# Far passes of a two-buffer sort in four instructions, one rotation less, other counts of zero matmuls

## The chip, the cores and the metric

The kernel runs on one core of a Trainium2 chip. The metric is the device time of one execution in microseconds (us). Before the change three runs took 396.53, 396.72 and 397.1 us; the median is 396.72.

## The reference

4096 nodes have 256 features each. Each of 262144 edges carries its source node's features, times a weight matrix, to its target node, where they are summed; each node's own features, times a second matrix, are added.

```python
self_out = nodes @ w_self
src_feat = nodes[edges_src]
msg = src_feat @ w_msg
agg = np.zeros((N, D), dtype=np.float32)
np.add.at(agg, edges_dst, msg)
return (self_out + agg).astype(np.float32)
```

## The kernel before

Nothing is gathered edge by edge. Each edge becomes one key, and the keys are sorted by a shell sort on the chip until each chunk of 128 edges touches one block of sources and a narrow window of targets. The main stage, from about 150 us on, makes one-hot matrices of the chunks on VectorE (DVE), multiplies them on TensorE (PE) into counts per block and window (`ring`), evicts these on ScalarE (ACT) and multiplies them with the projected nodes `Y` into `out_ps`. Two tables of 2048 numbers each, `WID` and `GAP`, give the columns that each chunk's window may take; they follow from the sort's amounts.

The sort holds 128 x 2048 keys in one of two buffers, `XA[0]` and `XA[1]`, and goes from one to the other. A pass with a distance m compares each key of every second block with the key m further on in the same partition: one DVE instruction writes the minima and one the maxima (`mm`, line 1156). Two passes of the same m, with parity 0 and 1, are a pair. Pairs of m over 96 (`FP`) are far passes, the others near passes. `SORT_A` (line 202) lists the passes, and between them rotations (`'q'`).

- Far passes: `far_gap` (line 1237) does a pair in seven DVE instructions and leaves untouched blocks where they are, in a buffer that it writes in part. ACT has no part in it. `far_pass` (line 1258) is not reached, since all far passes come in pairs.
- Near passes: `near` (line 1212) does all pairs between two rotations. It cuts the passes into waves, so that the first half of the array is ready for the next rotation while DVE still works on the second. It also calls `warm`.
- Rotations: `rotate` (line 1275) turns each half by 8 groups of matmuls with a shifted identity, in three PSUM tiles, each copied back by ACT. The next near passes start on the first half when it has been copied.
- `warm` (line 1162) puts groups of n zero matmuls (128 x 512) into PE's order ahead of the next rotation, each made to wait for the DVE instruction that lies a given span before the point at which the first half is ready. `WARM` (line 176) has for each rotation the spans and n.

The order of each engine is the order of the code (`manual_schedule`); waits are on semaphores that the framework derives from the data. Work that the sort doesn't need is put between its parts by a generator, `early` (line 487): 16 steps that transpose the nodes (four matmuls into `x_ps` and a cast to `XT`), then 32 projections into `Y` and 16 of the nodes' own rows (two matmuls into `y_ps` and a copy each). `FILLS` (line 178) says how many steps come ahead of the sort and behind each rotation. `x_ps` and `y_ps` share two PSUM buffers. After the sort come a transposition (`relayout`), a tail of 14 near passes on each half of the keys (one half at once, the other beside the main stage), and the main stage.

Of the kernel before, what the change touches and what calls it, by code (L numbers as in the profile page):

```python
# [11 lines left out]
P = 128  # L12
# [160 lines left out]
BEFORE, AFTER = 0, 2  # L173
FP = 96
BP = 128
WARM = [((6.0, 4.8, 3.6, 2.4, 1.2), 3)] + [((2.7, 1.4), 3)] * 8
TURNED = ((0, 4), (4, 2), (6, 2))
FILLS = (24, 10, 10, 10, 0, 5, 0, 0, 5)
LAG = (16, 84)
# [83 lines left out]
def kernel(  # L263
# [86 lines left out]
    j = 0  # L350
# [148 lines left out]
    for _ in range(FILLS[0]):  # L499
        next(fill)  # L500
# [902 lines left out]
```

## Time and profile before

| | |
|---|---|
| median of three runs | 396.72 us |
| profiled execution: time / span | 396.69 / 394.8 us |
| DVE busy | 356.4 us (90%) |
| PE busy | 321.8 us (82%) |
| ACT busy | 261.2 us (66%) |
| POOL busy | 77.9 us (20%) |
| mean granted PE clock | 0.985 |

Busy times are of the whole span; the stages differ. In the sort and its tail, to about 145 us, DVE is busy nearly all the time. In the main stage PE, DVE and ACT share the work, and PE has the most of it. The clock is that of PE, as a share of full speed.

### The profile page before, as it was taken

Reading aid. Unit: us, or ns where it says so; the run is one execution under the profiler, and the core shown is the slowest. Engines: PE = TensorE matmul, PEld = TensorE weight load, DVE = VectorE, ACT = ScalarE, POOL = GpSimd, SP = SyncE. Lnnn points to the kernel's source line nnn. Section 1 sums busy time; section 2 is a strip of 40 time slices with the busy share of each in tenths; the row PEclk is TensorE's granted clock in tenths of the full one; section 3 lists DMA queues with packets and bytes.
Section 4 is the critical chain, followed back from the end, with each engine's and each line's share of the span. In section 5 each row is a group of like instructions: output and inputs, shape, how many; then the busy total and the mean of one; then the engine's idle time right before and its main releaser. Section 6 shows DMA issues by size and latency. Waiting matters only on the chain.

```text
span 394.8 us, 11312 instructions
## 1 busy us (share of the span) xinstructions
PE 321.8 (82%) x4147; PEld 274.1 (69%) x4157; DVE 356.4 (90%) x616; ACT 261.2 (66%) x571; POOL 77.9 (20%) x1088
## 2 busy tenths in 40 slices
PE   0028688886967188998999899999999999999985
PEld 0016256664746054987898798989999989999974
DVE  5999999999999998899999999979999899999350
ACT  4418155533447105868897879999888888888862
POOL 5499950000000100000200202120212020211001
PEclk9999999999999779999999999999999999999999
DMA  8691000011032400000301202221121112121204
GB/s 302 155 185 28 3 2 0 5 49 55 1 107 69 146 0 2 2 2 2 42 2 16 28 2 30 56 38 21 17 29 18 25 17 30 15 28 18 28 2 71
DMA packets 17731, 16.26 MB, mean 41 GB/s; under 512 B 3334, under 2 KB 16647, under 8 KB 17674
## 3 DMA queue, kind: packets, MB, share of 16 engines
q0 software_dynamic: 8992, 6.29, 13.4%
q1 hardware_dynamic: 7962, 7.22, 5.3%
q10 hardware_dynamic: 720, 2.00, 1.4%
q8 instruction: 34, 0.56, 0.6%
q14 instruction: 23, 0.19, 0.2%
HBM read 8.93 MB, written 8.67 MB: 45 GB/s over the span
## 4 chain that ended last, share of the span: by engine, by line
DVE 45%; PE 45%; ACT 5%; issue 2%; DMA 1%; ACTq 0%; DVEq 0%
PE out_ps L890 21%; DVE XA L1158 20%; PE ring L795 17%; DVE oh L766 9%; DVE XR L1158 6%; DVE XS L1158 4%; DVE off L729 3%; PE tp_sw L1284 3%; PE warm L1178 3%; ACT XA L1288 2%; ACT atr L823 2%; DMA d<-in_edges_dst_dram 1%; PE out_ps L897 1%; DVE XA L392 1%; DVE XA L387 1%
## 5 line engine op out<-in xcount | busy, mean ns | idle before, releaser
L823 ACT CAST atr<-ring 128x468 bf16<-128x468 f32 (+15 forms) x352 | 170.2, 559 | 30.7 <-PE ring L795 30.2
L890 PE MATMUL out_ps<-Y,atr 128*128 128x256 bf16 x1024 | 149.9, 272 | 0.6 <-ACT o_sb L907 0.5
L766 DVE TENSOR_SCALAR oh<-off 128x2560 bf16<-128x2560 int16 (+8 forms) x209 | 132.9, 694 | 8.4 <-PE ring L795 6.2
L795 PE MATMUL ring<-oh 128*128 128x70 bf16 (+23 forms) x2048 | 112.4, 197 | 7.0 <-issue 4.5
L795 PEld LDWEIGHTS <-oh 128*128 128x128 bf16 x2048 | 104.5, 98 | 15.6 <-issue 8.3
L890 PEld LDWEIGHTS <-atr 128*128 128x128 bf16 x1024 | 97.1, 98 | 7.7 <-issue 0.2
L1158 DVE TENSOR_TENSOR XA<-XA 128x510 f32<-128x510 f32 (+32 forms) x154 | 89.4, 631 | 2.5 <-ACT XA L1288 0.5
L795 PE MATMUL ring<-zer 128*128 128x156 bf16 (+13 forms) x352 | 80.9, 231 | 1.1 <-ACT atr L823 0.9
L1048 POOL DMA_DIRECT2D out_dram<-o_sb x30 | 32.9, 1130 | 217.0 <-ACT atr L823 217.0
L1288 ACT COPY XA<-tp_sw 128x256 f32<-128x256 f32 (+1 forms) x48 | 19.8, 450 | 37.5 <-PE tp_sw L1284 37.2
L1284 PE MATMUL tp_sw<-XA,id 128*128 128x128 f32 x256 | 32.4, 278 | 6.8 <-DVE XA L1158 6.3
L729 DVE TENSOR_TENSOR off<-pair,rows 128x2560 int16<-128x2560 int16 (+5 forms) x28 | 37.6, 1344 | 0.3
L1284 PEld LDWEIGHTS tp_sw<-XA,id 128*128 128x128 f32 x256 | 30.0, 190 | 11.2 <-DVE XA L1158 9.0
L795 PEld LDWEIGHTS <-zer 128*128 128x128 bf16 x358 | 34.6, 97 | 2.7 <-ACT atr L823 1.4
L1178 PE MATMUL warm<-zw 128*128 128x512 bf16 x78 | 23.7, 412 | 15.3 <-DVE XS L1158 9.1
L443 POOL MEMSET prow<- 1x1 f32 x1024 | 33.9, 89 | 1.2 <-issue 1.2
L479 PE MATMUL x_ps<-id_bf,nodes_bf 128*128 128x128 bf16 x64 | 8.5, 303 | 28.7 <-DMA nodes_bf<-in_nodes_dram 27.5
L897 PE MATMUL out_ps<-Y,atr 128*82 128x256 bf16 (+9 forms) x115 | 31.3, 272 | 0.0
L754 ACT ACTIVATE oh<-off,onesc 128x640 bf16<-128x640 uint16 (+5 forms) x30 | 22.7, 760 | 8.6 <-DVE off L729 7.2
L479 PEld LDWEIGHTS <-nodes_bf 128*128 128x128 bf16 x64 | 6.6, 139 | 30.4 <-DMA nodes_bf<-in_nodes_dram 27.8
L1178 PEld LDWEIGHTS <-zw 128*128 128x128 bf16 x87 | 8.0, 101 | 27.6 <-DVE XS L1158 9.4
L451 PE MATMUL y_ps<-wcat,XT 128*128 128x256 bf16 x128 | 22.3, 286 | 5.6 <-ACT Y L455 2.2
(115 smaller groups left out, 231.4 us busy)
## 6 DMA issues: line engine op xcount, KB each, us to landing
out_dram<-o_sb POOLq DMA_DIRECT2D x30, 128.0 KB, 3.3
nodes_bf<-in_nodes_dram POOLq DMA_DIRECT2D x2, 1024.0 KB, 12.3
out_dram<-nodes_bf SPq DMA_DIRECT2D x4, 512.0 KB, 3.8
out_dram<-XA SPq DMA_DIRECT2D x4, 512.0 KB, 3.1
s<-in_edges_src_dram ACTq DMA_DIRECT2D x2, 512.0 KB
d<-in_edges_dst_dram SPq DMA_DIRECT2D x2, 512.0 KB, 5.4
s<-in_edges_src_dram ACTq DMA_DIRECT2D x1, 480.0 KB, 9.2
d<-in_edges_dst_dram SPq DMA_DIRECT2D x1, 480.0 KB, 9.4
```

Of the source, the lines that this page charges most:

```text
L443: nc.gpsimd.memset(words[:, z0:z1], float(packed[z0]))
L729: tt(out=v[:, 0:n // 2].rearrange("p g w (k i) -> p (g w) k i", i=2), in0=pair[:, g].rearrange("p g w i -> p (g w) i").unsqueeze(2).to_bro ...
L766: ins = tss(out=bass.AP(tensor=dst.tensor, offset=dst.offset, ap=[list(row), [2 * WE, n // 2], [2 * P, both], [1, 2 * NW]],), in_=v[:, 0:n ...
L795: mm = nc.tensor.matmul(out=ap, lhsT=lhsT, rhs=rhs, start=start, stop=True, skip_group_check=True,).ins
L823: ins = nc.scalar.copy(out=atr[:, i:i + k, 0:n], in_=_view3(ring[:, b:b + k * BW], BW)[:, :, 0:n]).ins
L890: nc.tensor.matmul(out=out_ps[:, i, :], lhsT=at[:, t * P:(t + 1) * P], rhs=Y[:, b, :], start=(b == 0 and not last and t % 2 == 0), stop=(b ...
L897: nc.tensor.matmul(out=out_ps[0:m, 0, :], lhsT=spill[:, c0:c0 + m], rhs=Y[:, b, :], start=False, stop=False, skip_group_check=True,)
L1048: nc.gpsimd.dma_start(out=dst, in_=src, accum_op=ALU.add).ins,
L1158: self.nc.vector.tensor_tensor(out=out, in0=in0, in1=in1, op=op),
L1178: self.nc.tensor.matmul(out=w[:], lhsT=self.zw[:, 0:P], rhs=self.zw[:], start=True, stop=True).ins
L1284: self.nc.tensor.matmul(out=tp[:, g * P:(g + 1) * P], lhsT=self.turned(rots[8 * h + g0 + g]), rhs=sel(x)[:, g0 + g], start=True, stop=True,)
L1288: self.nc.scalar.copy(out=sel(y)[:, g0:g0 + n], in_=tp.rearrange("p (g i b) -> p g i b", g=n, b=bb),)
```

## The change

The far passes of a pair take four DVE instructions, each pass from one buffer to the other, and ACT copies the blocks that a pass does not touch. The 24 steps that stood ahead of the sort are gone; 18 steps come between far passes instead (`FIRST`: so many behind each first and each second pass), and 12, 12, 12, 0, 5, 0 and 5 behind the seven rotations, where there were 10, 10, 10, 0, 5, 0, 0 and 5 behind eight. The list of passes has one rotation less, with other distances and rotation amounts. `WARM` has 15 zero matmuls ahead of the first and the fourth rotation, 6 ahead of the second and third, and 9 ahead of the later ones and of the transposition (before: 15 ahead of the first, 6 ahead of the others). `WID` and `GAP` are made anew (lines 32 to 163, not shown), and the tail's distances change a little.

```diff
-WARM = [((6.0, 4.8, 3.6, 2.4, 1.2), 3)] + [((2.7, 1.4), 3)] * 8
+WARM = [((6.0, 4.8, 3.6, 2.4, 1.2), 3)] + [((2.7, 1.4), 3)] * 2 + [((6.0, 4.8, 3.6, 2.4, 1.2), 3)] + [((4.0, 2.7, 1.4), 3)] * 4
-FILLS = (24, 10, 10, 10, 0, 5, 0, 0, 5)
+FIRST = ((0, 0), (0, 0), (2, 1), (2, 2), (2, 2), (2, 5))
+FILLS = (12, 12, 12, 0, 5, 0, 5)
...
 SORT_A = [
-    ('b', 743, 0),
-    ('b', 743, 1),
+    ('b', 727, 0),
+    ('b', 727, 1),
...
-    ('b', 299, 0),
-    ('b', 299, 1),
+    ('b', 261, 0),
+    ('b', 261, 1),
...
-    ('b', 53, 0),
-    ('b', 53, 1),
+    ('b', 49, 0),
+    ('b', 49, 1),
...
-    ('q', 2, [92, 4, 58, 90, 125, 14, 32, 46, 56, 120, 43, 67, 24, 45, 38, 49]),
     ('b', 5, 0),
     ('b', 5, 1),
...
-    for _ in range(FILLS[0]):
-        next(fill)
-    sort.run({i: [fill] * n for i, n in enumerate(FILLS[1:])}, halo // P)
+    sort.run(
+        {i: [fill] * n for i, n in enumerate(FILLS)}, halo // P,
+        [([fill] * i, [fill] * n) for i, n in FIRST],
+    )
...
-    def far_gap(self, x, y, m):
+    def far_gap(self, x, y, m, more):
 
         b = m & -m
-        n = (2048 - m) // b
-        k = (2048 - 2 * m) // b
...
+        q, k = m // b, 2048 // b
+        n = k - q
+        at = lambda v, i, c: _blocks(v, FP + i * b, c, b)
+        for par, a, z in ((0, x, y), (1, y, x)):
+            for i, end in ((1 - par, q), (n + (n + par) % 2, k)):
+                c = (end - i + 1) // 2
+                if c > 0:
+                    self.nc.scalar.copy(out=at(z, i, c), in_=at(a, i, c))
+            c = (n + 1 - par) // 2
+            for to, op in ((par, ALU.min), (par + q, ALU.max)):
+                self.mm(at(z, to, c), at(a, par, c), at(a, par + q, c), op)
+            for f in more[par]:
+                next(f, None)
...
-                    self.far_gap(x, y, op[1])
-                    j += 1
-                else:
-                    self.far_pass(x, y, *op[1:3])
-                x, y = y, x
+                assert ops[j + 1] == ("b", op[1], 1)
+                self.far_gap(x, y, op[1], between.pop(0))
+                j += 1
```

After the change the pairs between rotations are: 49; 57 and 39; 37 and 13; 13, 9 and 5; 5 and 3; 2; 2; 2 and 1. Before they were 53; 57 and 39; 33 and 13; 13 and 9; 5; 5 and 2; 2; 2; 2 and 1.

The far passes of distance 245 on DVE, before, from the pair's first instruction to the first of the next pair:

```order
L1158 TENSOR_TENSOR XA_93<-XA_92 128x902 [waits DVE_49]
L1158 TENSOR_TENSOR XA_92<-XA_92 128x779 [waits DVE_49]
L1158 TENSOR_TENSOR XA_93<-XA_92 128x123
L1158 TENSOR_TENSOR XA_93<-XA_92,XA_93 128x779 [waits DVE_49] x2
L1158 TENSOR_TENSOR XA_93<-XA_92 128x122 x2
L1158 TENSOR_TENSOR XA_92<-XA_93 128x875 [waits DVE_49]
```

The same after, and the pair behind it:

```order
L1159 TENSOR_TENSOR XA_93<-XA_92 128x902 [waits DVE_49,Activation_49]
L1159 TENSOR_TENSOR XA_93<-XA_92 128x902
L1159 TENSOR_TENSOR XA_92<-XA_93 128x901 [waits DVE_49,Activation_49]
L1159 TENSOR_TENSOR XA_92<-XA_93 128x901
L1159 TENSOR_TENSOR XA_93<-XA_92 128x894 [waits DVE_49,Activation_49]
```

Seven instructions became four, and the first of each pass now waits for ACT as well. What ACT has at the same place after (before it had nothing there), `XT` being the transposed nodes:

```order
L1248 COPY XA_93<-XA_92 128x122 [waits DVE_49,Activation_49]
L1248 COPY XA_93<-XA_92 128x122 [waits Activation_49]
L484 CAST XT<-x_ps 128x512 [waits PE_49] x2
L1248 COPY XA_92<-XA_93 128x123 [waits DVE_49,Activation_49]
L1248 COPY XA_92<-XA_93 128x123 [waits Activation_49]
L484 CAST XT<-x_ps 128x512 [waits PE_49]
```

The copies of the second pass stand behind two casts of the first. The steps behind the fifth rotation on ACT, before (`nodes_bf` takes the nodes' own rows; the segment behind this rotation has two pairs):

```order
L1288 COPY XA_93<-tp_sw 128x4x64x2
L1288 COPY XA_93<-tp_sw 128x2x64x2 x2
L455 COPY nodes_bf<-y_ps 128x256 x5
L1288 COPY XA_92<-tp_sw 128x4x64x2
L1288 COPY XA_92<-tp_sw 128x2x64x2 x2
```

On PE after, the end of those steps and the first of the nine zero matmuls that lie between them and the sixth rotation (the segment has one pair):

```order
L451 LDWEIGHTS XT
L451 MATMUL y_ps<-wcat,XT 128x256 [waits Activation_49]
L451 LDWEIGHTS XT
L451 MATMUL y_ps<-wcat,XT 128x256
L1179 LDWEIGHTS zw
L1179 MATMUL warm<-zw 128x512
```

Ahead of this piece stand the fifth rotation and eight more matmuls on `y_ps`; behind it eight more zero matmuls and then the sixth rotation. Before the first rotation PE has after the change the 64 matmuls on `x_ps`, 4 on `y_ps`, 15 zero matmuls and then the rotation, with the last five steps (12 and 4 matmuls) coming behind the last far pair in the code.

## Rows read from the trace of the kernel before

**Rows 1.** Busy time by stages: us, then each engine's busy us (and instructions), clock, DMA.

```profile
core 0: us, PE busy (x) PEld busy (x) DVE busy (x) ACT busy (x) POOL busy (x), PEclk, DMA share, GB/s
19.09:45.84 26.75, 14.97 (x88) 9.23 (x89) 26.20 (x42) 11.58 (x24) 25.54 (x768) 1.00 0.61 80
150.50:394.80 244.30, 229.46 (x3558) 209.91 (x3558) 215.19 (x364) 197.79 (x415) 32.95 (x30) 1.00 0.17 22
```

**Rows 2.** The chain of waits in order of time: start us, us, engine, tile, line.

```profile
48.68 2.07 PE tp_sw L1284 x16
51.17 1.31 DVE XA L1158 x2
72.28 1.30 DVE XA L1158 x2
...
82.72 1.31 DVE XA L1158 x2
84.04 1.45 DVE XA L1158 x4
85.50 0.81 PE warm L1178 x3
86.31 0.91 PE tp_sw L1284 x8
...
88.53 1.31 DVE XA L1158 x2
...
104.81 1.30 DVE XA L1158 x2
110.50 1.30 DVE XA L1158 x2
...
120.87 1.09 DVE XS L1158 x2
```

**Rows 3.** DVE in the far passes: two pieces of the timeline, then one form.

```profile
24.97 1.72 DVE L1158 TENSOR_TENSOR XA<-XA,XA 128x661 f32<-128x661 f32 x2
26.61 0.34 DVE L1158 TENSOR_TENSOR XA<-XA 128x181 f32<-128x181 f32 x1
...
L1158 DVE TENSOR_TENSOR XA<-XA 128x976 f32<-128x976 f32 x1 | 1.2, 1175 | 0.0
```

**Rows 4.** ACT instructions by form: count, busy us, mean ns.

```profile
L380 ACT ACTIVATE XS<-s 128x320 int32<-128x320 int32 x1 | 0.5, 489 | 0.0
...
L484 ACT CAST XT<-x_ps 128x512 bf16<-128x512 f32 x16 | 8.6, 587 | 14.4 <-PE x_ps L479 14.4
```

**Rows 5.** PE in order of time: start us, us, instructions, idle time before.

```profile
27.13 1.04 PE L479 MATMUL x_ps<-id_bf,nodes_bf 128*128 128x128 bf16 x8 [27.13 <-DMA nodes_bf<-in_nodes_dram]
...
67.81 1.46 PE L1178 MATMUL warm<-zw 128*128 128x512 bf16 x5
...
84.64 1.67 PE L1178 MATMUL warm<-zw 128*128 128x512 bf16 x6
...
90.30 0.60 PE L451 MATMUL y_ps<-wcat,XT 128*128 128x256 bf16 x4
...
92.04 0.38 PE L451 MATMUL y_ps<-wcat,XT 128*128 128x256 bf16 x2 [0.18 <-ACT nodes_bf L455]
```

**Rows 6.** One projection matmul early and late, stretches with their clock, zero matmuls in the chain.

```profile
L451 PE MATMUL y_ps<-wcat,XT 128*128 128x256 bf16 x16 | 4.2, 396 | 0.2 <-ACT XT L484 0.2
...
L451 PE MATMUL y_ps<-wcat,XT 128*128 128x256 bf16 x70 | 11.3, 270 | 3.0 <-ACT Y L455 2.2 <-ACT nodes_bf L455 0.9
...
37.44:41.65 4.21, 4.21 (x16) 1.88 (x15) 4.14 (x7) 3.05 (x8) 4.21 (x131) 1.00 0.01 2
...
142.00:145.00 3.00, 2.94 (x15) 1.60 (x13) 2.90 (x8) 0.00 (x0) 0.00 (x0) 0.67 0.00 0
...
139.07 1.50 PE warm L1178 x3
140.61 1.88 PE warm L1178 x4
```

More of the change, by code (lines that the diff above doesn't have):

```diff
@@ L214 @@
     ('b', 97, 1),
-    ('b', 53, 0),
-    ('b', 53, 1),
-    ('q', 32, [48, 124, 17, 36, 46, 5, 29, 78, 91, 77, 58, 48, 93, 119, 70, 29]),
+    ('b', 49, 0),
+    ('b', 49, 1),
+    ('q', 32, [97, 0, 30, 122, 19, 5, 43, 20, 110, 83, 43, 105, 112, 114, 42, 117]),
     ('b', 57, 0),
@@ L221 @@
     ('b', 39, 1),
-    ('q', 16, [103, 49, 25, 81, 79, 41, 99, 24, 109, 87, 93, 65, 12, 97, 124, 100]),
-    ('b', 33, 0),
-    ('b', 33, 1),
+    ('q', 16, [16, 90, 64, 88, 26, 123, 103, 53, 18, 36, 57, 125, 64, 20, 33, 122]),
+    ('b', 37, 0),
+    ('b', 37, 1),
     ('b', 13, 0),
     ('b', 13, 1),
-    ('q', 8, [64, 98, 61, 40, 90, 105, 84, 96, 37, 109, 8, 98, 85, 1, 73, 53]),
+    ('q', 8, [22, 13, 31, 24, 20, 42, 15, 38, 31, 27, 72, 29, 114, 46, 77, 87]),
     ('b', 13, 0),
@@ L231 @@
     ('b', 9, 1),
-    ('q', 2, [92, 4, 58, 90, 125, 14, 32, 46, 56, 120, 43, 67, 24, 45, 38, 49]),
     ('b', 5, 0),
     ('b', 5, 1),
-    ('q', 2, [94, 66, 0, 22, 34, 43, 21, 8, 91, 54, 17, 48, 77, 126, 107, 110]),
+    ('q', 2, [51, 71, 35, 122, 18, 76, 77, 90, 36, 14, 125, 20, 113, 97, 74, 69]),
     ('b', 5, 0),
     ('b', 5, 1),
+    ('b', 3, 0),
+    ('b', 3, 1),
+    ('q', 2, [61, 59, 95, 74, 115, 38, 15, 36, 29, 107, 17, 113, 71, 38, 34, 14]),
     ('b', 2, 0),
     ('b', 2, 1),
-    ('q', 2, [75, 114, 65, 39, 70, 28, 26, 123, 71, 83, 23, 104, 113, 97, 107, 116]),
+    ('q', 2, [102, 108, 15, 24, 33, 125, 60, 47, 95, 57, 96, 81, 114, 0, 82, 11]),
     ('b', 2, 0),
     ('b', 2, 1),
-    ('q', 2, [30, 21, 42, 26, 124, 18, 46, 105, 41, 12, 69, 24, 13, 120, 105, 108]),
-    ('b', 2, 0),
-    ('b', 2, 1),
-    ('q', 2, [83, 103, 41, 42, 46, 64, 127, 29, 48, 62, 69, 119, 46, 36, 101, 93]),
+    ('q', 2, [83, 62, 81, 98, 125, 59, 89, 116, 1, 113, 30, 75, 48, 50, 102, 6]),
     ('b', 2, 0),
@@ L250 @@
     ('b', 1, 1),
-    ('q', 1, [26, 61, 77, 96, 120, 64, 116, 57]),
+    ('q', 1, [83, 68, 6, 9, 56, 33, 27, 62]),
 ]
 SORT_S = [
-    (77, 0), (77, 1), (55, 0), (55, 1), (39, 0), (39, 1), (25, 0), (25, 1), (15, 0), (15, 1), (13, 0), (13, 1), (8, 0), (8, 1),
+    (83, 0), (83, 1), (51, 0), (51, 1), (31, 0), (31, 1), (29, 0), (29, 1), (17, 0), (17, 1), (15, 0), (15, 1), (8, 0), (8, 1),
 ]
@@ L1235, in near @@
         return x, y
-    def far_gap(self, x, y, m):
+    def far_gap(self, x, y, m, more):
         b = m & -m
-        n = (2048 - m) // b
-        k = (2048 - 2 * m) // b
-        for par in (0, 1):
-            cnt, cin = (n + 1 - par) // 2, max(0, (k + 1 - par) // 2)
-            s, f = FP + par * b, FP + (par + 2 * cin) * b
-            if par == 0:
-                self.mm(
-                    _blocks(y, s, cnt, b), _blocks(x, s, cnt, b), _blocks(x, s + m, cnt, b), ALU.min
-                )
-            for i, (st, c) in enumerate(((s, cin), (f, cnt - cin))):
-                if not c:
-                    continue
-                lo = _blocks(x, st, c, b)
-                up = _blocks(y if par == 1 and i == 0 else x, st + m, c, b)
-                if par == 1:
-                    self.mm(_blocks(y, st, c, b), lo, up, ALU.min)
-                self.mm(_blocks(x if par == 0 and i == 0 else y, st + m, c, b), lo, up, ALU.max)
-    def far_pass(self, x, y, m, par):
-        b = m & -m
-        n = ((2048 - m) // b + 1 - par) // 2
-        s = par * b
-        low, up = _blocks(x, FP + s, n, b), _blocks(x, FP + s + m, n, b)
-        for st in ((1 - par) * b, s + 2 * n * b):
-            end = m if st < m and st == (1 - par) * b else 2048
-            c = -(-(end // b - st // b) // 2)
-            if c > 0:
-                self.nc.scalar.copy(out=_blocks(y, FP + st, c, b), in_=_blocks(x, FP + st, c, b))
-        self.mm(_blocks(y, FP + s, n, b), low, up, ALU.min)
-        self.mm(_blocks(y, FP + s + m, n, b), low, up, ALU.max)
+        q, k = m // b, 2048 // b
[11 more added lines that the diff above has]
+                next(f, None)
     def turned(self, r):
@@ L1291, in rotate, with run @@
                 )
-    def run(self, fill, more):
+    def run(self, fill, more, between):
         nc = self.nc
@@ L1312, in run @@
             if op[0] == "b":
-                if op[2] == 0 and j + 1 < len(ops) and ops[j + 1] == ("b", op[1], 1):
-                    self.far_gap(x, y, op[1])
-                    j += 1
-                else:
-                    self.far_pass(x, y, *op[1:3])
-                x, y = y, x
+                assert ops[j + 1] == ("b", op[1], 1)
+                self.far_gap(x, y, op[1], between.pop(0))
+                j += 1
             elif op[0] == "q":
```

256 rows, old and new, of tables (GAP, WID) are left out of this document.

## The prediction

> **What bounds the kernel now.** Read first the table by stages: DVE is busy 26.20 of the 26.75 us of the far passes (19.09 to 45.84), and from 150.50 on PE works 229.46 of 244.30 us [rows 1]. So the sort up to 120.87, where the tail's first pass starts, is a chain on DVE, and what is won or lost in it moves all that follows. Read then the chain of waits, in order of time: it stays on DVE and leaves it only at rotations (PE turns half of the array, ACT copies it back, DVE goes on) [rows 2]. I call the near passes between two rotations a segment: before, A has one pair of passes, B, C and D two, E one, F two, G and H one, I two. B starts at 51.17, E at 82.72, F at 88.53, the tail at 120.87 [rows 2]. In a segment of one pair the chain already runs through zero matmuls: in E the first half was ready at 85.50 (the DVE piece at 84.04 took 1.45), but the rotation started at 86.31, behind three zero matmuls of 0.81 [rows 2]. PE works in the order of the program, so the forecast turns on what stands in PE's order ahead of each rotation.
>
> **Far passes.** Before, a pair takes seven DVE instructions, after it four, over about as many elements. From 24.97 two instructions that both wait take 1.72, so the second started 0.87 after the first, each lasting some 0.85 for 661 elements; one that waits for the one ahead follows 0.02 behind its end, one that doesn't starts 0.08 before it (26.61, 0.77 after the second) [rows 3]. With 1.175 for 976 elements [rows 3] an element costs (1.175 - 0.85)/315 = 1.03 ns. The new sizes are 661, 843, 902, 894, 943 and 976, so one instruction takes 0.85, 1.04, 1.10, 1.09, 1.14 and 1.18; a pair takes four of these less 0.12: 3.28, 4.03, 4.27, 4.24, 4.44 and 4.58, together 24.84. Against 26.75 that is **-1.9 us**, A starts at 43.93.
>
> The cover of it: the blocks that a pass doesn't touch are now copied by ACT, two copies a pass. The largest have 364 elements; an ACT instruction of 320 takes 0.49 [rows 4], so two take about 1.1 beside two DVE instructions of 0.85. The later ones have 48 to 182 elements, under 0.49 each, with one or two casts of 0.59 [rows 4] behind them in passes of 2.1 to 2.3 us. I cost them at nothing. What is queued behind: the copies of a second pass stand behind the casts of the first, and these need the nodes, whose first matmul came at 27.13 [rows 5]. The third pair, with the first of these casts, starts at 26.40, its second pass at 28.55; first casts at 27.8 and 28.4 end near 28.9, and their copies are needed only at the fourth pair, 30.67. That leaves about 1 us. Bounds: 0, and 2 us lost if the nodes came so much later.
>
> **Segment A.** The transposes and two projections that stood in PE's order before the sort now come between far passes, the last five after the last pair; behind them stand 15 zero matmuls, then the rotation. ACT can cast the last five only after the copies of the second pass, which wait for the first pass of the last pair, over at 39.35 + 2.29 = 41.64. Copies to about 42.1, casts at 0.54 to 0.59 each, two PSUM buffers: PE issues the last of the five at about 44.4 (44.0 to 44.8). Then come five groups of three zero matmuls. Such a group takes 0.81 at the full clock [rows 2]. At the half clock a group of four took 1.88, from 140.61 [rows 6], so three take 1.88 - 0.43 = 1.45 (0.43 being 512 columns at 1.2 GHz). Which clock? The granted clock reads 1.00 from 37.44 to 41.65 [rows 6], but the same projection matmul of 256 columns lasts 396 ns there and 270 ns from 50 on [rows 6]; I take the early stretch as half clock (1.2 GHz) in spite of that row. PE was busy 4.21 of those 4.21 us before it sped up [rows 6]. Later, after PE had idled, zero matmuls began at 139.07 at half clock, and the full clock came back in the stretch 142 to 145 (mean 0.67, so at about 144, 4.9 us after they began) [rows 6]. After the change PE does in 27 to 44 less per us than before, so I expect it to be at half clock at 44.4. With 4.9 us of that, 3.4 groups of 1.45 and 1.6 of 0.82 take 6.2 us; the rotation starts at 50.6.
>
> The Trainium skill (TensorE: Matmul & The Clock Gate, Part 1: The HAM clock gate) says that the throttled clock is the default and that activity releases it; the durations of 396 and then 270 ns agree, the recorded 1.00 does not. By the record the five groups take 4.1 us and the rotation starts at 48.5; by the rule it is the 50.6 above.
>
> From a rotation that PE starts late to the next segment's start it takes 88.53 - 86.31 = 2.22 us [rows 2]. B starts at 52.8, where it started at 51.17: **+1.65 us** net, the far gain included. DVE itself has done A's first half 2.84 us after A's start (45.84 to 48.68 before [rows 1, 2]), at 46.8. Bounds for the rotation: 48.5 with the full clock throughout, 51.7 with all five groups at 1.45. So B moves by -0.45 to +2.7.
>
> **Rotation less.** After the change the segments are A one pair, B and C two, D three, E two, F and G one, H two. Two pairs last 10.44 (72.28 to 82.72), one lasts 5.81 or 5.69 (E, and H from 104.81 to 110.50) [rows 2]. A third pair in D adds four undivided instructions of some 1028 elements, 4 x 1.23 - 0.12 = 4.8, so D lasts 15.2. Two pairs and one (10.44 + 5.75) become 15.2: **-1.0 us**.
>
> **What stands in front of the rotations behind them.** At the full clock, which these rows show:
> - C: two more projections ahead of the zero matmuls, which started at 67.81 [rows 5]. Four projections took 1.74 (90.30 to 92.04), so two take 0.87, and six zero matmuls 1.67 [rows 5]; PE is free at 70.35, and + 2.22 is 72.57 where D started at 72.28: **+0.3**. In B the same comes out even. Bounds 0 and +0.8.
> - F has one pair now, and the five projections that stood ahead of a segment of two pairs stand ahead of it, with nine zero matmuls instead of six. In F of before PE began projections at 90.30, 1.77 after the segment's start, and the last group at 92.04 took it to about 92.4, 3.86 after the start [rows 5]. Nine zero matmuls: in E six took 84.64 to 86.31, 1.67 [rows 2, 5], nine take 2.48. The rotation starts 6.34 after the segment, the next segment 8.56 after it, where a segment of one pair lasts 5.75: **+2.8**. DVE then sits idle, since it is done after some 5.7.
> - G: nine zero matmuls and no projections. PE ends the second half of the rotation 1.63 to 1.93 after the segment's start (in E 84.64 - 82.72 = 1.92), + 2.48 + 2.22 = 6.3 to 6.6: **+0.55**.
> - E and H have two pairs and D three, so their zero matmuls end before the half is ready: nothing. Bounds for F and G together: 0, if PE's order did not hold the rotation back, and +3.7.
>
> **Tables and sizes.** The new widths sum to 147342 columns against 146937, 405 more, at 2.4 GHz 0.17 us of PE; with wider cleared zones and slightly longer tail passes (18400 elements against 18312 a half) I take **+0.35**, bounds 0 and +0.7.
>
> **Sum.** +1.65 - 1.0 + 0.3 + 2.8 + 0.55 + 0.35 = +4.65. The profiled execution took 396.69 (span 394.8), the median is 396.72, so there is nothing to convert: 396.69 + 4.65 = **401.3 us**.
>
> **The rivals.**
> 1. *The clock is full when the 15 zero matmuls start.* For it: the recorded 1.00 [rows 6]; against it: 396 against 270 ns. Segment A then gives -0.45 instead of +1.65: 399.2.
> 2. *The rotations are not held back, so the change gives what it takes away: faster.* The place is PE's order ahead of the first rotation and of F's and G's. It needs PE to be through projections and zero matmuls when DVE has half the array ready. Then -1.9 - 1.0 + 0.3 + 0.35 = -2.25: 394.4. It decides from the point where the work ahead of a rotation is shorter than DVE's first half: 3.1 us in a segment of one pair. Against it: the 0.8 us in E that six zero matmuls already cost [rows 2], and the order, in which nothing but weight loads stands between.
> 3. *ACT's copies become late.* If casts wait for nodes or for PE at half clock, DVE waits in the far passes too, once or in several pairs. The pass has some 1 us to spare; a miss of 0.5 in four pairs puts 2 us on A's start, and part of that would be hidden behind the zero matmuls: 402 to 403.5.
> 4. *It comes out even,* within 0.8 us of before: half of F's and A's delays missing.
>
> **How the numbers follow.** Forecast 0.57 (own range 400.6 to 402.4: the time at which the clock rises, 49.9 to 51.7 for the rotation being its ends), rival 1 0.19, rival 3 0.11, rival 4 0.06, rival 2 0.07. The range 398.8 to 403.2 takes in rival 1 and most of 3. 0.2%, or 0.8 us, is about what a measurement of this kernel can tell from no change. Faster 0.07, within it 0.06, slower 0.87.
>
> **What would show it.** The chain after should have the first far passes in four instructions, A starting near 43.9; then DVE idle before B by 3 us or so, with PE's zero matmuls as the releaser, the first of them lasting longer than the last; DVE idle again by 2.5 to 3 us ahead of G, and about 0.6 ahead of H; the tail starting near 125. Projections that end before 44 or a first rotation at 47 would prove segment A wrong; a segment F of 5.8 us would prove the largest term wrong. If DVE waits for ACT's copies in the far passes, their cover was costed wrongly.

## The result and the profile after

The changed kernel takes 401.92 us (median of four runs, 400.57 to 402.31), the kernel before 396.62 on the same chip (396.42 to 397.10): 1.0125 times as long, 95% interval 1.0104 to 1.0146. The forecast was 401.3. The profiled execution is the shortest of the four, 400.57 us with a span of 398.7, so its trace shows 3.9 us of the loss.

Busy time by stages, with the columns of [rows 1]: the far passes, the segments up to the tail's first pass, the main stage.

```profile
18.80:44.72 25.92, 9.35 (x68) 7.22 (x69) 24.64 (x24) 14.75 (x40) 24.98 (x752) 1.00 0.62 83
44.72:123.88 79.16, 64.14 (x412) 43.36 (x410) 72.17 (x117) 33.87 (x93) 9.07 (x276) 1.00 0.08 28
153.87:398.70 244.83, 229.70 (x3558) 210.05 (x3558) 215.36 (x363) 197.90 (x415) 33.40 (x30) 1.00 0.16 22
```

The far passes last 25.92 us instead of 26.75 [rows 1], the segments 79.16 instead of 75.03 (45.84 to 120.87 [rows 1, 2]). DVE is busy for only 72.17 of these. The chain of waits shows what it waits for; these are the pieces that answer to [rows 2].

```profile
20.67 1.62 DVE XA L1159 x2
...
22.38 2.00 DVE XA L1159 x2
...
39.96 2.27 DVE XA L1159 x2
...
42.31 0.38 ACT XA L1248 x2
...
44.72 1.41 DVE XA L1159 x2
...
48.13 0.82 PE warm L1179 x3
...
49.00 0.81 PE warm L1179 x3
49.80 0.91 PE tp_sw L1267 x8
...
52.03 1.30 DVE XA L1159 x2
...
73.18 1.30 DVE XA L1159 x2
...
88.41 1.30 DVE XA L1159 x2
...
98.88 1.30 DVE XA L1159 x2
100.20 1.45 DVE XA L1159 x4
101.67 1.45 DVE XA L1159 x4
...
104.48 0.81 PE warm L1179 x3
105.29 3.57 PE tp_sw L1267 x32
...
111.24 0.90 PE tp_sw L1267 x8
...
113.52 1.31 DVE XA L1159 x2
...
123.88 1.08 DVE XS L1159 x2
```

The last copies on ACT (42.31) wait for the eleventh far pass (39.96), and PE's last steps wait for the casts behind these copies. The first rotation stands behind zero matmuls (49.80), and so do the one inside F (105.29) and the one inside G (111.24). What DVE loses is in its timeline: in brackets the idle time ahead of the first instructions of B, G and H, and what ended it.

```profile
52.03 52.41 DVE L1159 TENSOR_TENSOR XA<-XA 128x511 f32<-128x511 f32 x80 [2.04 <-ACT XA L1271]
107.57 5.57 DVE L1159 TENSOR_TENSOR XA<-XA 128x510 f32<-128x510 f32 x12 [3.14 <-ACT XA L1271]
113.52 10.36 DVE L1159 TENSOR_TENSOR XA<-XA 128x510 f32<-128x510 f32 x16 [0.38 <-ACT XA L1271]
```

ACT is named, since it copies the rotation back, but it had waited for PE. PE's timeline gives the order ahead of the two rotations:

```profile
44.48 0.59 PE L451 MATMUL y_ps<-wcat,XT 128*128 128x256 bf16 x2 [0.19 <-ACT XT L484]
44.86 4.94 PE L1179 MATMUL warm<-zw 128*128 128x512 bf16 x15
49.64 3.73 PE L1267 MATMUL tp_sw<-XA,id 128*128 128x128 f32 x32
...
102.54 0.38 PE L451 MATMUL y_ps<-wcat,XT 128*128 128x256 bf16 x2 [0.18 <-ACT nodes_bf L455]
102.75 2.54 PE L1179 MATMUL warm<-zw 128*128 128x512 bf16 x9
105.13 1.05 PE L1267 MATMUL tp_sw<-XA,id 128*128 128x128 f32 x8
```

Behind 44.48 there is no gap in PE until 53.37: zeros and rotation follow at once, so PE's own queue is what the rotation waited for. The zeros are slow at first. Their mean in ns over 44 to 47.4, and then over 47 to 60:

```profile
L1179 PE MATMUL warm<-zw 128*128 128x512 bf16 x7 | 2.7, 487 | 0.1
...
L1179 PE MATMUL warm<-zw 128*128 128x512 bf16 x16 | 4.4, 377 | 0.2
```

### The profile page after: what moved, and what is told of

Read it like the earlier page. It is cut to its first block, busy times and chain, and to the rows that moved or that the text cites. A ratio compares the mean times of both kernels' runs of the same rounds, so it can differ in the third digit from the quotient of the medians.

```text
span 398.7 us, 11293 instructions
## 1 busy us (share of the span) xinstructions
PE 321.8 (81%) x4140; PEld 271.7 (68%) x4140; DVE 354.6 (89%) x590; ACT 264.6 (66%) x589; POOL 78.3 (20%) x1088
## 4 chain that ended last, share of the span: by engine, by line
PE 54%; DVE 38%; ACT 3%; issue 2%; DMA 1%; DVEq 0%; ACTq 0%
PE out_ps L891 25%; PE ring L796 21%; DVE XA L1159 19%; DVE XS L1159 6%; DVE oh L767 6%; PE tp_sw L1267 2%; DVE XR L1159 2%; PE warm L1179 2%; PE out_ps L898 2%; ACT XA L1271 1%; DMA d<-in_edges_dst_dram 1%; DVE off L730 1%; DVE XA L392 1%; DVE XA L387 1%; DVE XA L386 1%
## 5 line engine op out<-in xcount | busy, mean ns | idle before, releaser
L824 ACT CAST atr<-ring 128x468 bf16<-128x468 f32 (+17 forms) x352 | 170.3, 559 | 31.1 <-PE ring L796 30.9
L796 PE MATMUL ring<-oh 128*128 128x73 bf16 (+26 forms) x2048 | 112.5, 197 | 7.1 <-issue 4.2
L1159 DVE TENSOR_TENSOR XA<-XA 128x510 f32<-128x510 f32 (+28 forms) x140 | 96.8, 743 | 8.3 <-ACT XA L1271 5.6
L796 PE MATMUL ring<-zer 128*128 128x152 bf16 (+13 forms) x352 | 81.0, 232 | 1.4 <-ACT atr L824 1.2
L1271 ACT COPY XA<-tp_sw 128x256 f32<-128x256 f32 (+1 forms) x42 | 17.2, 449 | 36.9 <-PE tp_sw L1267 36.6
L1179 PE MATMUL warm<-zw 128*128 128x512 bf16 x102 | 29.6, 405 | 13.9 <-DVE XS L1159 8.8
L898 PE MATMUL out_ps<-Y,atr 128*84 128x256 bf16 (+9 forms) x115 | 31.3, 273 | 0.0
L1267 PE MATMUL tp_sw<-XA,id 128*128 128x128 f32 x224 | 27.7, 277 | 4.4 <-DVE XA L1159 3.9
L1267 PEld LDWEIGHTS tp_sw<-XA,id 128*128 128x128 f32 x224 | 26.2, 190 | 7.3 <-DVE XA L1159 4.1
L1179 PEld LDWEIGHTS <-zw 128*128 128x128 bf16 x102 | 9.6, 102 | 30.2 <-DVE XS L1159 9.5
```

The lines of the kernel that those rows point to most:

```text
L796: mm = nc.tensor.matmul(out=ap, lhsT=lhsT, rhs=rhs, start=start, stop=True, skip_group_check=True,).ins
L824: ins = nc.scalar.copy(out=atr[:, i:i + k, 0:n], in_=_view3(ring[:, b:b + k * BW], BW)[:, :, 0:n]).ins
L898: nc.tensor.matmul(out=out_ps[0:m, 0, :], lhsT=spill[:, c0:c0 + m], rhs=Y[:, b, :], start=False, stop=False, skip_group_check=True,)
L1159: self.nc.vector.tensor_tensor(out=out, in0=in0, in1=in1, op=op),
L1179: self.nc.tensor.matmul(out=w[:], lhsT=self.zw[:, 0:P], rhs=self.zw[:], start=True, stop=True).ins
L1267: self.nc.tensor.matmul(out=tp[:, g * P:(g + 1) * P], lhsT=self.turned(rots[8 * h + g0 + g]), rhs=sel(x)[:, g0 + g], start=True, stop=True,)
```

## The experiments

The theory: the loss is PE's queue ahead of the first rotation and of those in F and G, and what the far passes and the missing rotation give is lost behind it. The rivals: the zeros cost nothing and the loss lies elsewhere (in ACT's copies, the tables or the main stage), or PE's clock sets the time whatever stands in the queue. Each kernel was timed against the kernel before; edits are to the changed kernel unless said otherwise.

| kernel | median, us (runs) | ratio, 95% | B starts | tail starts | main starts, lasts |
|---|---|---|---|---|---|
| before | 396.62 (4) | | 51.17 | 120.87 | 150.75, 244.05 |
| changed | 401.92 (4) | 1.0125 [1.0104, 1.0146] | 52.03 | 123.88 | 153.87, 244.83 |
| k1 | 399.77 (5) | 1.0090 [1.0077, 1.0103] | 52.17 | 122.02 | 152.09, 245.01 |
| k2 | 403.00 (5) | 1.0175 [1.0162, 1.0188] | 52.26 | 122.98 | 152.95, 247.25 |
| k3 | 402.33 (6) | 1.0155 [1.0128, 1.0181] | 53.45 | 122.19 | 152.15, 247.95 |
| k4 | 401.54 (4) | 1.0125 [1.0110, 1.0140] | 52.14 | 124.89 | 154.85, 246.15 |
| k5 | 398.52 (6) | 1.0049 [1.0037, 1.0062] | 53.17 | 121.91 | 151.87, 245.13 |
| k6 | 397.51 (12) | 1.0029 [1.0018, 1.0040] | 50.2 | 120.42 | 150.44, 244.66 |
| k7 | 400.04 (5) | 1.0089 [1.0076, 1.0102] | 51.56 | 124.29 | 154.26, 245.04 |
| k8 | 396.40 (11) | 0.9997 [0.9988, 1.0006] | 50.1 | 119.18 | 149.16, 245.34 |
| k9 | 396.99 (11) | 1.0010 [1.0001, 1.0019] | | 120.53 | 150.40, 244.90 |
| k10 | 400.62 (5) | 1.0095 [1.0080, 1.0110] | 50.82 | 123.98 | 153.86, 244.54 |

The medians of the kernel before in the same comparisons lie between 396.45 and 396.62. Starts and lengths are of each kernel's profiled execution. The main stage is counted here from its first matmul, 150.75 for the kernel before, where [rows 1] starts it at 150.50.

**k1: the five projections from F to E.**

```diff
-FILLS = (12, 12, 12, 0, 5, 0, 5)
+FILLS = (12, 12, 12, 5, 0, 0, 5)
```

> The five projections behind the fifth rotation go behind the fourth, ahead of a segment of two pairs. If they and the nine zero matmuls hold back the sixth rotation (my theory), segment F falls from 8.69 to about 6.6 us (1.92 + 2.48 + 2.22) and G may rise from 5.95 to 6.3; the median falls by 1.5 to 2.1 us, to about 400. If F is long for another reason (copies of the rotation, DVE itself), F stays at 8.7 and the time within 0.5 us.

From B's start to the tail it takes 69.85 us instead of 71.85, and the median falls by 2.15. DVE's idle time ahead of G is 1.19, not 3.14:

```profile
105.71 5.56 DVE L1159 TENSOR_TENSOR XA<-XA 128x510 f32<-128x510 f32 x12 [1.19 <-ACT XA L1271]
```

The projections do the same work as before, in a segment of two pairs. Only their place in PE's order has changed, from ahead of F's rotation to ahead of E's, and that was worth 2 us.

**k2: six zero matmuls ahead of the rotations in F and G.** In `WARM`, turns 5 and 6 (counted from 0) get `((2.7, 1.4), 3)`.

> Six zero matmuls instead of nine in segments F and G only. By my theory F falls by one group, 0.82 us, to 7.8 to 7.9, G to about 5.6, and the median by about 1.2 us, to 400.7. The rival: nine were needed to keep PE at its full clock there; then the rotation matmuls of F to H last longer than 279 ns in the trace and the time does not fall.

In the sort the theory holds: B to tail takes 70.72, 1.13 less, with 2.27 us idle ahead of G and none ahead of H. Yet the median is 1.1 us above that of the changed kernel, since the main stage takes 2.4 us more. The chain there, in the trace of k2, has a piece in which PE waits for nothing that the profile shows:

```profile
323.79 1.64 PE out_ps L891 x15
325.43 1.92 issue
327.34 0.71 PE ring L796 x14
```

One microsecond inside it, by engines (columns of [rows 1], the DMA share being the last but one), and the one instruction fetch recorded from 318 to 329, which lies between 323 and 324 (packets, MB, share of 16 engines in that microsecond):

```profile
326.00:327.00 1.00, 0.00 (x0) 0.10 (x1) 1.00 (x3) 0.00 (x0) 0.00 (x0) 1.00 0.94 116
```

```profile
q8 instruction: 1, 0.02, 8.4%
```

PE does nothing while the DMA engines are 94% busy adding a piece of the output, and an instruction fetch was recorded shortly before. My reading, an inference: PE waited for its own instructions. If so, where a fetch falls would depend on how many instructions PE has, and k2 has 12 fewer. The transfers alone don't stop PE: in the changed kernel it works through the same DMA load, also behind a fetch (between 326 and 327):

```profile
327.00:328.00 1.00, 0.99 (x19) 0.76 (x18) 1.00 (x3) 0.63 (x2) 0.28 (x1) 1.00 0.94 111
```

**k3: k1 and k2 together.**

> Both edits: F and G should both be what a segment of one pair was before the change, 5.7 to 5.8 us; DVE's idle time ahead of G and H falls from 3.5 to under 0.5 us; the median falls by 3.1 us, to 398.8. If the two edits had each only shifted the wait, the sum would be less than 2 us.

B to tail is 68.74, the whole 3.1 us expected. Two things take it away. The main stage lasts 247.95, with gaps as in k2 (0.94 before 293.82, 1.13 and 0.62 between 325 and 327). And the 15 zeros of A, the same code as in the changed kernel up to there, took 6.17 us instead of 4.94 (4.95 in k1, 5.29 in k2), as the chain's groups show:

```profile
45.25 1.29 PE warm L1179 x3
...
46.59 1.45 PE warm L1179 x3
...
48.08 1.43 PE warm L1179 x3
...
49.55 0.82 PE warm L1179 x3
...
50.41 0.81 PE warm L1179 x3
51.22 0.91 PE tp_sw L1267 x8
```

So the moment at which the zeros speed up differs between executions, by more than a microsecond. That the median of the changed kernel lies 1.35 above its profiled run may be this; of the runs without a profile nothing shows it.

**k4: three zeros instead of 15 ahead of the first rotation,** `WARM[0] = ((1.2,), 3)`.

> One group of three zero matmuls ahead of the first rotation instead of five. By my theory PE is free by 46.3 and the rotation starts when DVE has half the array, near 47.5 (49.8 with five groups), so B starts near 49.8 instead of 52.0 and the median falls by 2.2 us or more; the spread of the runs (400.6 to 402.3) shrinks if it comes from the moment at which the clock rises among the 15. The rival: with so few zero matmuls PE is still at half clock in the rotation; then its matmuls last 400 ns or more, B starts at 51.5 or later, and the time falls by less than 1 us.

B starts no earlier (52.14). The rotation starts 1.8 us sooner, at 48.00, but at the half clock: 3.71 for 16 matmuls that take 2.05 to 2.07 at the full one [rows 2]. Mean ns of one from 47.9 to 52:

```profile
L1267 PE MATMUL tp_sw<-XA,id 128*128 128x128 f32 x19 | 4.4, 430 | 0.0
```

Here the rival on the clock was right: taking the zeros away gives nothing, since PE pays in the rotation what it saved. It then paid again: the rotation at 96.51, in E, ran at the half clock too (4.56 for 24), and the tail starts 1.0 later than in the changed kernel.

The main stage of k4 is 1.3 us longer than the changed kernel's. PE, with 24 instructions fewer, has three idle pieces there that no wait explains: 0.82 before 264.96, 0.53 before 265.84 and 1.03 before 328.80. At the first the DMA engines are nearly idle, so such a gap doesn't need the output's transfers:

```profile
264.00:265.00 1.00, 0.18 (x6) 0.05 (x3) 0.86 (x2) 1.00 (x4) 0.00 (x0) 1.00 0.03 2
```

**k5: k3 with six more zero matmuls behind the sort,** between the transposition and the main stage, where DVE is what is waited for. They bring PE's program back to the length that it has in the changed kernel (4140 weight loads in both traces; k3 has 4134).

```diff
+    sort.keep_warm(6)
```

> k3_both with six zero matmuls more at a place where PE has nothing to do (ahead of the tail's end), so that PE's program is again as long as in the changed kernel. If the gaps of PE in the main stage (1.92 us in k2_six, 3.2 us in three pieces in k3_both) come from where PE's program is fetched against the output's additions, they go, the main stage takes 244.8 to 245.0 us instead of 247.9, and the median falls to about 399, 3 us under the changed kernel's. If they come from the earlier start of the main stage, they stay, and the time stays at 402.

The main stage is 245.13 again, and the median falls by 3.8 us against k3. Of PE's idle pieces that no wait explains, the longest is now 0.72 (before 223.67), and the kernel before has one of 0.71 at the same place. Instructions that compute nothing and run over 160 us before the gaps thus take them away. The other kernels with the changed sort fit: with 4140 weight loads (the changed one, k1, k5 to k8) no such piece is longer than 0.72, with 4134 or 4128 (k2, k3, k4) the longest are 1.92, 1.13 and 1.03. So PE's program ahead of the main stage decides, most likely by its length. That this works through the fetch is argued, not shown.

**k6: the queue ahead of the first rotation emptied.** k1, and five steps fewer come behind the last far pair, five more behind the third rotation (in D); the rotation that ends D gets six zeros, and nine zeros stand behind the sort, where k5 has six.

```diff
-FIRST = ((0, 0), (0, 0), (2, 1), (2, 2), (2, 2), (2, 5))
-FILLS = (12, 12, 12, 0, 5, 0, 5)
+FIRST = ((0, 0), (0, 0), (2, 1), (2, 2), (2, 2), (2, 0))
+FILLS = (12, 12, 17, 5, 0, 0, 5)
```

> k1_moved with the last five steps moved from the last far pair to behind the third rotation (17 there), six zero matmuls ahead of the fourth rotation, and nine spare zero matmuls in PE's idle time to keep the program's length. PE is then free for the 15 zero matmuls from about 41.5 instead of 44.9. My theory: the clock comes up some 4.9 us after they begin, the first rotation starts near 47.7 at the full clock, B near 50.0 (52.2 in k1_moved), and the median falls by 2 us, to about 397.8. The rival: the clock needs the steps ahead of them as well, PE stays at half clock and B starts at 52 as in k4_one; then the time stays at 399.8.

B starts at 50.2 with no idle time ahead of it, and the tail at 120.42, 3.5 before that of the changed kernel. Without the five steps PE begins the zeros at 41.80, and is through with them when the first half is ready.

**k7: the old seven instructions in the far passes,** with no copies on ACT, all else as changed (`far_gap` of before; its result stays in the other buffer, so `x, y = y, x` behind it).

> The changed kernel with the far passes in seven DVE instructions as before and no copies on ACT. By my theory the casts no longer wait for DVE, PE is through the 18 steps by about 41, the zero matmuls are done when DVE has the first half, and B starts near 51.1 instead of 52.0: faster by 0.9 us or more, although the far passes themselves take 0.8 us longer. The rival, that the shorter far passes are worth their 0.8 us on the path: slower by 0.8 us.

The far passes last some 26.9 us again, and yet the median is 1.9 us below that of the changed kernel. B starts at 51.56. Without copies in ACT's queue the casts don't wait for DVE, PE has its last step done at 38.4 instead of 45.1, and the zeros can begin at 42.93, most of them at the half clock. The chain of k7 runs through them:

```profile
42.93 1.07 PE warm L1179 x2
...
44.05 1.45 PE warm L1179 x3
...
45.54 1.45 PE warm L1179 x3
...
47.03 1.45 PE warm L1179 x3
...
48.53 0.81 PE warm L1179 x3
49.33 1.80 PE tp_sw L1273 x16
```

DVE's idle time ahead of B falls to 0.19. So the shorter far passes gave nothing at B's start: with copies in ACT's queue PE gets its last steps later, and DVE arrives sooner at a rotation that PE begins when its own queue is through. The size of the gain in the median is not accounted for: in k7's profiled execution the tail starts 0.4 later than in the changed kernel's, as the rotation ahead of F ran at the half clock there (1.44 us idle at 99.76, as in k4).

**k8: k6 with six zeros in F and G too,** two steps moved from C to D, and fifteen zeros behind the sort.

> k6_free with six zero matmuls in segments F and G and two steps moved from C to D. F and G give 1.1 us and C 0.1: 396.6, within 0.3 us of the kernel before, if the main stage stays at 245.0. If the main stage again has gaps of 2 to 3 us, near 399.

It comes out as the kernel before, 0.9997. The sort is now what the change could give: the tail starts 1.69 us earlier than before, and DVE is idle twice for 0.33. The main stage, 1.29 longer, takes most of this back:

```profile
149.16:394.50 245.34, 230.13 (x3557) 210.09 (x3558) 215.48 (x363) 198.01 (x415) 32.00 (x30) 1.00 0.17 22
```

**k9: the kernel before, each chunk's window one column wider** (`WID = [n + 1 for n in WID]`), 2048 columns more where the change has 405.

> The kernel before with every window one column wider: 2048 columns more in the count matmuls, five times the 405 that the change adds. By the term of my sum (0.35 us for 405 columns with cleared zones) the main stage grows from 244.05 by 1 to 1.7 us. If the widths are what made the changed main stage 0.8 us longer, by about 4 us. Under 0.5 us: the widths cost next to nothing, and the 0.8 us have another cause.

The main stage takes 0.85 us more in the profile, the median 0.46. A fifth of that, 0.1 to 0.2 us, is what the changed widths can cost; they don't explain its 0.78. The zones that the main stage clears, 228 columns more after the change by the traces, are as before here.

**k10: the kernel before, with nine zeros instead of six ahead of the rotations in E, G and H.**

> The kernel before with nine zero matmuls instead of six in its three segments of one pair (E, G and H), nothing else. By my theory each holds its rotation back by one more group, 0.82 us: the tail starts 2.0 to 2.4 us later than 120.78, with DVE idle of some 1 us ahead of F, H and I where it was 0.25. The rival, that zero matmuls only fill time in which PE waits: no change in the sort.

The tail starts 3.1 us later, and the median is 4.1 higher. The rotation in E starts at 86.82, behind a third group (at 86.31 in [rows 2]), and DVE is idle for 1.11 ahead of F. E, G and H, the segments with more zeros, are 0.88, 0.32 and 0.55 longer, together 1.75 and not the 2.0 to 2.4 expected: that is what the zeros cost in a segment's length. F is 1.72 longer, and that comes from the clock, which fell there (stretches 88 to 94 and 94 to 100; the clock is the third number from the end), and a rotation there took nearly twice its time:

```profile
88.00:94.00 6.00, 3.97 (x33) 3.29 (x33) 4.89 (x8) 3.81 (x11) 0.00 (x0) 1.00 0.26 90
94.00:100.00 6.00, 5.17 (x19) 3.34 (x18) 5.31 (x9) 0.63 (x2) 0.00 (x0) 0.52 0.00 0
```

```profile
96.94 3.79 PE tp_sw L1284 x16
```

## Why the prediction was right

Its mechanism holds: what stands in PE's order ahead of a rotation moved the sort's end. k1, k2, k3 and k6 take such work away and get the time back in the sort, k10 adds it to the kernel before and loses it. Ahead of the first rotation PE's clock is part of it: k4 takes zeros away there and gains nothing. The terms, in the profiled executions:

| step | predicted | measured | from |
|---|---|---|---|
| length of the far passes (contained in the next row) | -1.9 | -0.83 | 26.75 to 25.92 |
| B's start, net of that | +1.65 | +0.86 | 51.17 to 52.03 |
| B and C | +0.3 | +0.04 | 21.11 to 21.15 |
| one rotation less (D) | -1.0 | -1.02 | 10.44 + 5.81 to 15.23 |
| E and F (before F and G) | +2.8 | +2.88 | 16.28 to 19.16 |
| G (before H) | +0.55 | +0.26 | 5.69 to 5.95 |
| tail, tables, main stage | +0.35 | +0.89 | 0.11 + 0.78 |
| sum | +4.65 | +3.9 | H adds -0.01 |

The sum in the trace is 0.75 us below the forecast, and the median lies 1.35 above the profiled execution, which no trace explains. That the forecast is within 0.6 us of the median is in part luck.

- **Far passes: mis-sized.** The instructions last what was assumed, but a pass whose first instruction waits for ACT too starts 0.09 us behind the end of the pass ahead (22.38 - 20.67 - 1.62), where I had put the 0.02 of a wait for DVE alone. Twelve times 0.07 is 0.84 of the 1.08 us missed; the first pass gave 0.15 more. The loss goes on into B's start, since the casts wait behind copies that wait for the eleventh pass: that was over at 42.24 instead of the 41.64 forecast, and the zeros began 0.46 later than forecast. Rival 3 is wrong: the copies were done in time, and only the form of the wait cost something.
- **Segment A: right, too large.** The last step was done, and the zeros began, at 44.86 (said 44.4), and the early ones were the slow ones (487 ns, then 377). They took 4.94 us instead of 6.2: by 1.45 and 0.82 a group that is 1.3 slow groups of five, where I had put 3.4. The rotation started at 49.80 instead of 50.6. k3, with the same code up to there, has 6.17, or 3.3 slow groups. So the size varies between executions, within the bounds given. The two misses, 0.46 later and 1.26 shorter, partly cancel.
- **Rival 1 is wrong.** The recorded clock reads 1.00 throughout 44.72 to 123.88, but the zeros' durations show the half clock, and in k4 the rotation itself runs at it. The Trainium skill (TensorE: Matmul & The Clock Gate, Part 1: The HAM clock gate) takes the throttled clock as the default; the durations agree, the record does not.
- **Rotation less and F: right** within 0.1 us. F lasts 8.69 (said 8.56), and k1 alone gives back 2.0 of it.
- **G: half of the term.** Its rotation starts behind the zeros, and DVE idles 0.38 instead of some 0.6. C's +0.3 was not there.
- **Main stage: mis-sized, the cause open.** It is 0.78 us longer. The widths (405 columns) and the cleared zones (228) come to some 0.26 at k9's 0.85 for 2048, an estimate. Gaps like those of k2 to k4 are not the rest: PE's idle pieces of over 0.5 us that no wait explains are 0.65 and 0.71 (before 196.94 and 225.80), and the kernel before has 0.69 and 0.71 (before 193.68 and 222.44). Where the other 0.5 us arise was not separated.
- **Rival 2, faster,** failed at the point it named, PE's queue longer than DVE's first half. Even without that queue, as k8 has it, the change is worth nothing that can be measured: 1.7 us in the sort, 1.3 lost in the main stage.

## What to carry to other kernels

Work that is put into the idle time of an engine that runs in order stands ahead of whatever comes next on that engine. Before adding it, add up the queue ahead of each handover and compare it with the time until the handover's data are ready; where segments differ in length, put it into the long ones. And shortening a stage is worth nothing as long as the engine that it hands over to comes through its own queue later.

## What the runs showed that was not expected

- PE's clock can fall in the middle of the sort: after a stretch in which PE was busy 3.97 of 6.00 us it was granted 0.52 (k10), while in the kernel before 4.18 of 6.00 us at the same place were followed by 1.00; what sets it off is not shown. Half an array turned at the half clock took 1.6 to 1.7 us more (k4, k10).
- In the first 50 us the recorded clock of 1.00 does not tell the clock; the duration of one known matmul does (487 and then 377 ns for the same zero matmul, all at a recorded 1.00).
- A dozen instructions fewer on PE went with 2.4 us more in a main stage whose own code was unchanged (k2), and as many that compute nothing took such gaps away (k5). Why is not shown.
